# Five reorderings in a hybrid S5 and windowed-attention layer: key products by half tiles, a key power behind a query's, gated columns two units sooner, two scratch buffers swapped, a PSUM ring shifted by one

## The chip, the cores and the metric

The kernel runs on one core of a Trainium2 chip, in one launch. The metric is the device time of that launch in microseconds (us). Three runs gave a median of 1460.14 us (1459.45 to 1464.28). One further execution was profiled; it took 1461.13 us, of which the trace spans 1459.3 us, so that 1.83 us lie around the span.

## The reference, cut to what matters

One encoder layer is computed for two sequences of 512 tokens (width 1024), all in float32. Cut to its data flow:

```python
h = rms_norm(x, ln1)
q, k, v, u, g_att, g_ssm = jnp.split(h @ w_in, IN_SPLITS, axis=-1)
q, k = rms_norm(q per head of 64, q_gain), rms_norm(k per head of 64, k_gain)   # 16 query heads, 4 key heads
y_att = windowed_attention(q, k, v, sink, bias, mask)      # blocks of 128, a block sees its two neighbours
y = gelu(s5(u))                                            # bidirectional state space, 64 groups of 16
y_ssm = y * sigmoid(y @ w_glu + b_glu)
x = x + (sigmoid(g_att) * y_att + sigmoid(g_ssm) * y_ssm) @ w_out
out = x + square(relu(rms_norm(x, ln2) @ w_up)) @ w_down   # inner width 4096
```

## The kernel before, in words

Every float32 product is made of three passes on TensorE (PE): each operand is split into a rounded high part (a CAST on ScalarE, ACT) and the remainder (a subtraction on VectorE, DVE), and high x high, high x low and low x high are added up in one bank of PSUM (`mm3`, L119 to L123). A weight that comes in by DMA can therefore be multiplied only after its CAST and its subtraction. Splits have names in pairs: `c_hi`/`c_lo`, `gc_hi`/`gc_lo`, `w_hi`/`w_lo`, `act0`/`act1`.

The program is one long order written out by hand. Inside a `manual_schedule` the named engines take their instructions exactly in the order of the code; engines that are not named are ordered by a scheduler. All engines take their queues in order, so that an instruction that waits holds back all that stands behind it. Where a DMA is issued from SyncE's queue (SP), the same holds: an issue that waits for a free buffer holds back the issues behind it.

**PSUM before the up phase.** Eight banks: three in the ring `acc()` (L84), two each for `tps` and `sps`, one for `po`. A fourth `acc()` waits until the first one's readers are done. In the up phase (from L1530) the eight banks are handed out again as one ring, `bank()` (L1532).

**The stages the change touches**, in order of time:

1. *Front.* A small product `line` (L509 to L510) takes the bank of `po`, at about 51 us.
2. *Keys of the second half of the tokens* (`key_products`, L219 to L252; 400 to 411.6 us). Four tiles t = 4 to 7 of 128 tokens; each has 24 matmuls of 256 columns into one bank. The key weights come in two halves of 512 columns each, `loaded[len(columns)]` and the next; the second half is split while the first tile runs (`split` at n = 2 and 6). After a tile, ACT squares it (L239), DVE sums (L241), GpSimd (POOL) takes the power -1/2 (L243, L244), and DVE multiplies the keys in the following tile (`later`, L247).
3. *First queries* (L1108 to L1133; 413 to 438 us). For four tiles t = 0 to 3 (T0 to T3 below): the query projection of 24 matmuls (L914), ACT's square (L920), DVE's sum (L924), POOL's add and power (L926, L927), DVE's scaling of the bank to `qn` (L931), four transposes (L936), and the values' product of the same rows (L121 to L123 through `rows_block`). Each tile takes three banks of `acc()` in turn, so a tile's projection goes into the bank of the tile before, and must wait for that tile's `qn`. Between the tiles lies the norm of the first keys, which come back from DRAM: ACT's square `k_sq` (L1120), DVE's sum `k_ms` (L1121), POOL's add and power to `k_rs` (L1122, L1123; 16 numbers a row where a query tile has four), DVE's product with the keys (L1125), POOL's copy `kd` (L883), and four transposes at t = 2 (L896). POOL is not in the manual order here.
4. *Attention* in 8 steps (to about 684 us).
5. *Gated units* (L1305 to L1344; 684 to 754 us). 16 units u; unit u is sequence s = u % 2 of column block m = u // 2. A unit has 24 matmuls (`glu_step`, L128) with the columns of block m, and a string of DVE and ACT work (L804 to L831). The columns of a block come in two pieces (`column_half`, L794), DMA into `c_raw`, CAST to `gc_hi` (L780), subtraction to `gc_lo` (L781). The table `columns` (L1311) says in which unit a piece is loaded and split: blocks 4 to 7 in units 3, 4, 7, 8, 9, 10, 11, 12. The pairs `gc_hi`/`gc_lo` have two buffers, so that block 6's pair takes the place of block 4's. From unit 7 on, the rows of `w_out` are loaded and split as well (`w_raw`, L1297; L1302, L1303).
6. *Out phase* (754 to 856 us). Products with `w_out` (`out_half`), DVE adds `x` (L1376), then the norm: ACT's square (L1393), POOL's power (L1396), DVE's scaling `rn_xn` (L1402), transposes (L1418) for the up phase. Its last products are two pairs of `first_products` for the up phase, read out to `f_sum` (L1449, L1451).
7. *Up phase*, from 856 us: a fast matrix product of seven half-size products a round (L1575 on).

## Time and profile before

| what | value |
|---|---|
| median of three runs | 1460.14 us (1459.45 to 1464.28) |
| profiled execution, its own time | 1461.13 us |
| span of its trace | 1459.3 us |
| around the span | 1.83 us |
| mean granted TensorE clock | 0.999 of full |
| busy DVE, ACT, POOL | 1098.9, 764.3, 236.2 us |
| HBM traffic | 169.02 MB read, 81.82 MB written, 172 GB/s over the span |

A row of the timeline has the start in us, the duration, the engine, the line in the kernel, the operation, output and inputs, the shape, a count of merged instructions, and in brackets the idle time of that engine just before with what ended it. Matmuls overlap: the distance from one start to the next tells the pace, and the duration is longer. A row of the waits has engine, output and line that waited, the engine, output and line waited for, and then the total in us, how often and the longest. A row of the windows has the stretch, its length, each engine's busy time, the granted clock and the DMA share with its rate.

### The profile page before, as it was taken

How to read it: one execution, taken by the hardware profiler on the slowest of the kernel's cores; microseconds unless marked ns; L12 is line 12 of the kernel's file. 1: busy time of each engine (PE TensorE's matmuls, PEld its weight loads, DVE VectorE, ACT ScalarE, POOL GpSimd, SP SyncE). 2: the span in 40 equal slices, each digit the busy share in tenths (PEclk: the TensorE clock that was granted, in tenths of full speed). 3: DMA queues.
4: the chain of work that ended last, by engine and by line, in shares of the span. 5: the costliest groups of instructions: out<-in, count | busy, mean ns of one | idle time of the engine just before them, and what ended most of it. 6: DMA issues, size and time to landing. Idle time of an engine off the chain costs nothing.

```text
span 1459.3 us, 22019 instructions
## 1 busy us (share of the span) xinstructions
PE 1439.5 (99%) x7981; PEld 1226.0 (84%) x7981; DVE 1098.9 (75%) x1985; ACT 764.3 (52%) x1361; POOL 236.2 (16%) x386
## 2 busy tenths in 40 slices
PE   8999999999999999999999999999999999999998
PEld 6788888889999999987788878888888888888887
DVE  6999949995457999988975588777776598475654
ACT  7688861234338887884443355545445444333332
POOL 3144452004244432251100000000000000000000
PEclk9999999999999999999999999999999999999999
DMA  7356549428741533345553245444442993554441
GB/s 277 112 166 182 186 132 340 171 108 291 259 165 47 171 102 102 125 139 173 179 184 114 95 144 183 157 151 144 152 143 103 342 325 111 159 187 147 128 130 58
DMA packets 102204, 240.23 MB, mean 165 GB/s; under 512 B 12330, under 2 KB 25130, under 8 KB 102096
## 3 DMA queue, kind: packets, MB, share of 16 engines
q1 hardware_dynamic: 62160, 139.68, 29.4%
q0 software_dynamic: 16320, 48.28, 10.2%
q10 hardware_dynamic: 23616, 50.87, 9.3%
q8 instruction: 63, 1.03, 0.3%
q14 instruction: 45, 0.37, 0.1%
HBM read 169.02 MB, written 81.82 MB: 172 GB/s over the span
## 4 chain that ended last, share of the span: by engine, by line
PE 87%; DVE 6%; ACT 3%; DMA 1%; issue 1%; POOL 1%; DVEq 0%; ACTq 0%; SPq 0%; POOLq 0%
PE acc L190 16%; PE bank L122 14%; PE bank L121 14%; PE bank L123 14%; PE acc L914 5%; PE acc L123 2%; PE acc L121 2%; PE acc L122 2%; PE acc L128 2%; PE sps L748 2%; PE po L997 2%; PE sps L636 2%; PE sps L965 2%; PE tps L981 2%; PE acc L343 1%
## 5 line engine op out<-in xcount | busy, mean ns | idle before, releaser
L190 PE MATMUL acc<-act,c_hi 128*128 128x512 f32 x768 | 244.1, 395 | 0.0
L122 PE MATMUL bank<-b_lo,a_hi 128*128 128x512 f32 (+1 forms) x449 | 174.7, 389 | 0.0
L123 PE MATMUL bank<-b_hi,a_lo 128*128 128x512 f32 (+1 forms) x449 | 174.5, 389 | 0.0
L121 PE MATMUL bank<-b_hi,a_hi 128*128 128x512 f32 (+1 forms) x449 | 174.5, 389 | 0.0
L190 PEld LDWEIGHTS acc<-act,c_hi 128*128 128x128 f32 x768 | 142.4, 188 | 28.1 <-ACT act L316 0.9
L1649 ACT CAST a_hi<-d_a 128x1024 fp32r<-128x1024 f32 x56 | 59.1, 1055 | 177.9 <-PE bank L122 176.2
L190 PE MATMUL acc<-act,c_lo 128*128 128x512 f32 x384 | 151.2, 394 | 0.0
L121 PE MATMUL bank<-act,act 128*128 128x512 f32 x368 | 143.2, 389 | 2.1 <-ACT act L1410 2.1
L122 PE MATMUL bank<-act,act 128*128 128x512 f32 x368 | 143.2, 389 | 0.0
L123 PE MATMUL bank<-act,act 128*128 128x512 f32 x368 | 143.2, 389 | 0.0
L1650 DVE TENSOR_TENSOR a_lo<-d_a,a_hi 128x1024 fp32r<-128x1024 f32 x56 | 68.5, 1223 | 95.7 <-ACT a_hi L1649 95.7
L914 PE MATMUL acc<-w_hi,act 128*128 128x256 f32 x512 | 115.6, 294 | 1.7 <-DVE qn L931 1.7
L122 PEld LDWEIGHTS bank<-b_lo,a_hi 128*128 128x128 f32 x449 | 84.3, 188 | 18.3 <-DVE b_lo L1650 0.6
L121 PEld LDWEIGHTS bank<-b_hi,a_hi 128*128 128x128 f32 x449 | 84.3, 188 | 17.5
L123 PEld LDWEIGHTS bank<-b_hi,a_lo 128*128 128x128 f32 x449 | 84.3, 188 | 17.1
L914 PEld LDWEIGHTS acc<-w_hi,act 128*128 128x128 f32 x512 | 88.2, 192 | 5.7 <-DVE qn L931 1.9
L190 PEld LDWEIGHTS acc<-act,c_lo 128*128 128x128 f32 x384 | 72.2, 188 | 14.0 <-DVE c_lo L181 0.2
L121 PEld LDWEIGHTS bank<-act,act 128*128 128x128 f32 x368 | 69.1, 188 | 16.8 <-ACT act L1410 2.5
L975 ACT ACTIVATE p<-p,nmx 128x257 f32<-128x257 f32 (+1 forms) x128 | 72.1, 564 | 19.8 <-DVE nmx L969 17.6
L128 PE MATMUL acc<-act,gc_hi 128*128 128x512 f32 x256 | 81.2, 395 | 1.0 <-ACT gc_hi L780 1.0
L123 PEld LDWEIGHTS bank<-act,act 128*128 128x128 f32 x368 | 69.1, 188 | 14.5
L122 PEld LDWEIGHTS bank<-act,act 128*128 128x128 f32 x368 | 69.1, 188 | 14.2
(356 smaller groups left out, 3422.7 us busy)
## 6 DMA issues: line engine op xcount, KB each, us to landing
d_a<-a_scr SPq DMA_DIRECT2D x56, 512.0 KB, 3.6
raws<-in_w_up_dram SPq DMA_DIRECT2D x32, 512.0 KB, 4.1
a_scr<-t ACTq DMA_DIRECT2D x64, 256.0 KB, 3.0
k<-in_w_down_dram SPq DMA_DIRECT2D x32, 512.0 KB, 6.0
c_raw<-in_w_ug_dram SPq DMA_DIRECT2D x48, 256.0 KB, 3.6
ct_scr<-ctab POOLq DMA_DIRECT2D x16, 512.0 KB, 4.6
ctab_in<-ct_scr POOLq DMA_DIRECT2D x16, 512.0 KB, 6.3
a_scr<-a ACTq DMA_DIRECT2D x32, 256.0 KB, 2.0
```

Of the source, the lines that this page charges most:

```text
L121: PE.matmul(ps, a[0], b[0], start=first, stop=False)
L122: PE.matmul(ps, a[0], b[1], start=False, stop=False)
L123: PE.matmul(ps, a[1], b[0], start=False, stop=last)
L128: PE.matmul(ps, w[wi][:, k, :], rows[yi], start=k + p == 0, stop=k == KT - 1 and p == 2)
L190: PE.matmul(ps, w[wi][:, k, :], hT[s][hi][:, k, :], start=n == 0, stop=n == 3 * KT - 1)
L636: PE.matmul(ps[:, i * P:(i + 1) * P], bm[:, ri, g, :], u_sb[:, gp * SH + g, :], start=True, stop=True)
L748: PE.matmul(o, ctab[:, g0 % SI + g, ri, 0:T * CH], st[:, ri, g].rearrange("p s k -> p (s k)"), start=False, stop=ri == 1)
L914: PE.matmul(self.ps, hT[sq][act][:, k, col:col + P], w[:, k % 4, :], start=i == 0, stop=i == 3 * KT - 1)
L965: PE.matmul(ps[:, 0:self.nk], qs, kk[:, self.k0 * P:self.k1 * P], start=i == 0, stop=i == 1)
L975: S.activation(p, p, AF.Exp, bias=self.nmx[:, h:h + 1], scale=-1.0, accum_out=self.sums[:, h, self.qb:self.qb + 1])
L1649: S.copy(hi, src)
L1650: V.tensor_sub(lo, src, hi.bitcast(F32))
```

## The change

What it does, part by part:

- **Keys by half tiles.** Tile 4's first twelve matmuls, then tile 5's first twelve, then the second twelve of each; tiles 6 and 7 as before. Two banks are open at once. `later` comes at n = 17 instead of 12.
- **First keys' power behind a query's.** POOL joins the manual order of the query block, and the add and power of `k_ms`/`k_rs` are written at t = 1 instead of t = 0. With it `k_sq` takes a buffer of the tag `p` instead of `ya`.
- **Gated columns sooner.** Blocks 4 to 7 are loaded and split in units 3 to 10.
- **PSUM ring.** The product `line` takes a bank from `acc()`; the loops that called `acc()` and `bank()` without use, to bring the rings to a fixed place, go.

```diff
     def key_products():
-        later = None
-        for t in range(NB, NT):
-            if t == NB:
+        later, banks = None, {}
+        for t, half in ((4, 0), (5, 0), (4, 1), (5, 1), (6, 0), (6, 1), (7, 0), (7, 1)):
+            if not key_tiles:
                 key_tiles.append(evp.tile([P, 4, N_KV, HD], F32, tag="ev", name="keys"))
-            kt = key_tiles[-1][:, t % 4]
-            ps = acc()[:, 0:CB]
-            for n in range(3 * KT):
+            if not half:
+                banks[t] = acc()[:, 0:CB]
+            ps, kt = banks[t], key_tiles[-1][:, t % 4]
+            for n in range(half * 12, half * 12 + 12):
                 k, p = divmod(n, 3)
-                hi, lo = loaded[len(columns) + k // 4]
+                hi, lo = loaded[len(columns) + half]
...
-                if n == 12 and later:
+                if n == 17 and later:
                     later()
...
+            if not half:
+                continue
...
-        ps = ps_o.tile([P, 512], F32, tag="po", name="line")
+        ps = acc()
         PE.matmul(ps[0:N_HEADS, :], rel_sb, oh_sb, start=True, stop=True)
...
-        with tc.manual_schedule(engines={ET.PE, ET.DVE, ET.Activation}):
+        with tc.manual_schedule(engines={ET.PE, ET.DVE, ET.Activation, ET.Pool}):
...
-                    k_sq = ap.tile([P, NB, N_KV, HD], F32, tag="ya", name="k_sq")
+                    k_sq = ap.tile([P, NB, N_KV, HD], F32, tag="p", name="k_sq", bufs=3)
                     S.activation(k_sq, kn[:, 0:4], AF.Square, scale=HD ** -0.5)
                     V.reduce_sum(ms, k_sq.rearrange("p t h d -> p (t h) d"), axis=AX.X)
+                if t == 1:
                     GP.tensor_scalar_add(ms, ms, EPS)
                     GP.tensor_tensor(rk, ms, neg_half, op=ALU.pow)
-                if t == 1:
                     V.tensor_mul(kn[:, 0:4], kn[:, 0:4],
...
-        columns = {u: (4 + i // 2, i % 2) for i, u in enumerate((3, 4, 7, 8, 9, 10, 11, 12))}
+        columns = {u: (4 + i // 2, i % 2) for i, u in enumerate(range(3, 11))}
...
-        while banks_used[0] % 3 != 1:
-            acc()
...
-    for _ in range(6):
-        bank()
```

What the code's move makes of the engines' queues, at three places. First TensorE in the key products; `acc_4365` is the bank of tile 4, `c_hi_4179`/`c_lo_4180` the first half of the weights and `c_hi_4369`/`c_lo_4370` the second. Before, from tile 4's last matmul with the first half on:

```order
L230 MATMUL acc_4365<-c_hi_4179,act1_107 128x256
L230 MATMUL acc_4365<-c_hi_4369,act0_106 128x256
L230 MATMUL acc_4365<-c_lo_4370,act0_106 128x256
L230 MATMUL acc_4365<-c_hi_4369,act1_107 128x256
L230 MATMUL acc_4365<-c_hi_4369,act0_106 128x256
```

And in the change, where `acc_4384` is the bank of tile 5:

```order
L227 MATMUL acc_4365<-c_hi_4179,act1_107 128x256
L227 MATMUL acc_4384<-c_hi_4179,act0_106 128x256
L227 MATMUL acc_4384<-c_lo_4180,act0_106 128x256
L227 MATMUL acc_4384<-c_hi_4179,act1_107 128x256
...
L227 MATMUL acc_4365<-c_hi_4369,act0_106 128x256
L227 MATMUL acc_4365<-c_lo_4370,act0_106 128x256
```

Tile 5's twelve matmuls with the first half now stand between the two halves of tile 4.

Second GpSimd in the first queries, where a pair of `ms` and `rq` belongs to one query tile, from T0's power on. Before:

```order
L927 TENSOR_TENSOR rq<-ms,neg_half 128x4
L1122 TENSOR_SCALAR k_ms<-k_ms 128x16
L1123 TENSOR_TENSOR k_rs<-k_ms,neg_half 128x16
L926 TENSOR_SCALAR ms<-ms 128x4
L927 TENSOR_TENSOR rq<-ms,neg_half 128x4
L883 COPY kd<-kn 128x512
L926 TENSOR_SCALAR ms<-ms 128x4
```

And in the change:

```order
L926 TENSOR_TENSOR rq<-ms,neg_half 128x4
L956 COPY p<-vec 128x4
L925 TENSOR_SCALAR ms<-ms 128x4
L926 TENSOR_TENSOR rq<-ms,neg_half 128x4
L1122 TENSOR_SCALAR k_ms<-k_ms 128x16
L1123 TENSOR_TENSOR k_rs<-k_ms,neg_half 128x16
L882 COPY kd<-kn 128x512
L925 TENSOR_SCALAR ms<-ms 128x4
```

The keys' two instructions have changed places with T1's two; the copy `kd` still follows, ahead of T2's pair. The small copy `p` (a first attention unit's) comes between T0 and T1.

Third VectorE in units 4 to 7 of the gated stage, where a unit ends with its L831 and its pieces of weights follow. Before, from unit 4's end on:

```order
L831 TENSOR_TENSOR act_8302<-ga,act_8301 128x512
L781 TENSOR_TENSOR gc_lo<-c_raw,gc_hi 128x512
...
L831 TENSOR_TENSOR act_8304<-ga,act_8303 128x512
L825 TENSOR_TENSOR ga<-ga,gs 128x512
...
L831 TENSOR_TENSOR act_8302<-ga,act_8301 128x512
L825 TENSOR_TENSOR ga<-ga,gs 128x512
...
L831 TENSOR_TENSOR act_8304<-ga,act_8303 128x512
L781 TENSOR_TENSOR gc_lo<-c_raw,gc_hi 128x512
L1303 TENSOR_TENSOR act_8300<-w_raw,act_8299 128x512
```

And in the change:

```order
L830 TENSOR_TENSOR act_8302<-ga,act_8301 128x512
L780 TENSOR_TENSOR gc_lo<-c_raw,gc_hi 128x512
...
L830 TENSOR_TENSOR act_8304<-ga,act_8303 128x512
L780 TENSOR_TENSOR gc_lo<-c_raw,gc_hi 128x512
...
L830 TENSOR_TENSOR act_8302<-ga,act_8301 128x512
L780 TENSOR_TENSOR gc_lo<-c_raw,gc_hi 128x512
...
L830 TENSOR_TENSOR act_8304<-ga,act_8303 128x512
L780 TENSOR_TENSOR gc_lo<-c_raw,gc_hi 128x512
L1302 TENSOR_TENSOR act_8300<-w_raw,act_8299 128x512
```

Units 5 and 6 get a split each, block 5's; the split in unit 7 is now block 6's. ACT's casts and SP's loads of `c_raw` move along; units 11 and 12 lose theirs.

More of the change, by code (lines that the diff above doesn't have):

```diff
@@ L78, in hybrid_layer @@
     opers = ExitStack()
-    given = itertools.count()
-    banks_used = [0]
     def acc():
-        banks_used[0] = next(given) + 1
         return ps_acc.tile([P, 512], F32, tag="acc", name="acc")
```

## The prediction

> **What bounds the kernel now.** The page first: TensorE is busy almost throughout, so only time in which it stands still, or steps slowly, can be won.
>
> ```profile
> PE 1439.5 (99%) x7981; PEld 1226.0 (84%) x7981; DVE 1098.9 (75%) x1985; ACT 764.3 (52%) x1361; POOL 236.2 (16%) x386
> ```
>
> Of the 1459.3 us span that leaves 19.8 us of idle PE. The waits of PE say where, and the rows that bear on the change are these:
>
> ```profile
> PE bank L121 <- ACT act L1410: 2.1, 1, 2.1
> PE acc L914 <- DVE qn L931: 1.7, 1, 1.7
> PE acc L128 <- ACT gc_hi L780: 1.0, 1, 1.0
> PE acc L128 <- DVE gc_lo L781: 0.7, 1, 0.7
> ```
>
> Each happens once; together they make 5.5 us, and the two of the key products below add 0.6. A wait's idle time understates its cost, since the last matmul before it drains and the first ones after it step slowly; so I price by start-to-start distances in the timeline, less the usual step. A reading of this kernel tells about 0.3% (4.4 us) from no change.
>
> **Keys by half tiles.** The timeline of PE, ACT and DVE at the second half of the key weights:
>
> ```profile
> 401.26 0.28 PE L230 MATMUL acc<-c_lo,act 128*128 128x256 f32 x1
> 401.38 0.28 PE L230 MATMUL acc<-c_hi,act 128*128 128x256 f32 x1
> 401.92 0.38 PE L230 MATMUL acc<-c_hi,act 128*128 128x256 f32 x1 [0.26 <-ACT c_hi L180]
> 402.64 0.39 PE L230 MATMUL acc<-c_lo,act 128*128 128x256 f32 x1 [0.34 <-DVE c_lo L181]
> 402.87 0.41 PE L230 MATMUL acc<-c_hi,act 128*128 128x256 f32 x2
> 401.25 1.14 ACT L180 CAST c_hi<-c_raw 128x512 fp32r<-128x512 f32 x2 [0.40 <-ACT sg L205]
> 401.90 1.29 DVE L181 TENSOR_TENSOR c_lo<-c_raw,c_hi 128x512 fp32r<-128x512 f32 x2 [9.16 <-ACT c_hi L180]
> ```
>
> A step is 0.12 us (401.26 to 401.38). From 401.38 to 402.87 three steps take 1.49 us, 1.13 too much. In the change twelve matmuls of tile 5 lie in between, 12 x 0.12 = 1.44 us, so the second halves begin at 401.38 + 0.12 + 1.44 = 402.94. The first `c_lo` comes out half way through the DVE row of two, 401.90 + 0.65 = 402.55; the cover is enough by 0.4. The second is done at 403.19, and wanted six steps after the first. Gain 1.1 (between 0.9 and 1.1). Keys are now scaled five steps (0.6 us) later in a tile; the bank that this frees is wanted thirty matmuls (3.6 us) after it: nothing.
>
> **First keys' power behind a query's.** Timeline around T1 and T2, and the windows' row of the stretch behind:
>
> ```profile
> 421.68 2.92 POOL L1123 TENSOR_TENSOR k_rs<-k_ms,neg_half 128x16 f32<-128x16 f32 x1
> 421.96 0.42 DVE L924 TENSOR_REDUCE ms<-sq 128x4 f32<-128x256 f32 x1 [0.71 <-ACT sq L920]
> 424.54 0.28 PE L123 MATMUL acc<-w_hi,act 128*128 128x256 f32 x1
> 424.69 0.23 POOL L926 TENSOR_SCALAR ms<-ms 128x4 f32<-128x4 f32 x1
> 425.00 1.04 POOL L927 TENSOR_TENSOR rq<-ms,neg_half 128x4 f32<-128x4 f32 x1
> 426.07 0.42 DVE L931 TENSOR_TENSOR qn<-acc,rq 128x256 f32<-128x256 f32 x1 [3.69 <-POOL rq L927]
> 426.55 0.39 PE L914 MATMUL acc<-w_hi,act 128*128 128x256 f32 x1 [1.74 <-DVE qn L931]
> 427.64 1.22 DVE L1125 TENSOR_TENSOR kn<-kn,k_rs 128x1024 f32<-128x1024 f32 x1
> 428.78 1.22 DVE L1129 TENSOR_TENSOR va<-vn,va 128x1024 fp32r<-128x1024 f32 x1
> 429.00 1.47 POOL L883 COPY kd<-kn 128x512 f32<-128x512 f32 x1 [2.96 <-DVE kn L1125]
> 434.69 0.36 PE L914 MATMUL acc<-w_hi,act 128*128 128x256 f32 x1
> 427.60:431.02 3.42, 3.42 (x19) 3.40 (x18) 2.40 (x3) 0.00 (x0) 1.47 (x1) 0.50 0.00 0
> ```
>
> T1's sum is done at 422.38, but its power waits on POOL behind the keys' 2.92 us; so T2's first matmul, which needs T1's bank, starts 2.01 us after the last one, 1.89 too late. Right behind it the granted clock is 0.50 for 3.42 us: some 16 query matmuls at 0.21 instead of 0.12, about 1.5 us more. I put that down to the stop, which is the only one near.
>
> In the change, all 1.1 us earlier: sum done 421.3, add 0.3, power 1.04, `qn` at 422.65, and 0.48 later (as 426.07 to 426.55) T2 may start, 423.1; PE gets there at 424.54 + 0.12 - 1.1 = 423.56. No stop: 1.89 + 1.5 = 3.4 gained.
>
> What becomes late next is T2's own power. POOL now runs the keys' add and power from 422.65 to about 426.0; DVE's key product to 427.1, and behind it in DVE's queue the values' subtraction to 428.3; T2's sum stands behind both and ends at 428.7, though its projection is done by 426.5. POOL copies `kd` from 427.3 to 428.8, then T2's add and power end at 430.2, and T3 may start at 430.7. It is due at 423.56 plus the distance of T2 to T3 before without its slow clock, 434.69 - 426.55 - 1.5 = 6.6, so at 430.2: 0.5 us of new wait (0, if POOL and DVE hand over faster, to 1.0, if sum and copy do not overlap). `kd` itself is done at 428.8, one microsecond before its transposes. Net 2.9 (2.4 to 3.4). `k_sq` in `p` instead of `ya` adds no instruction; the buffer it takes held half of the values' weights, whose splits precede the first value product: nothing.
>
> **Gated columns sooner.** Timeline, and the windows' row of 700 to 740 us:
>
> ```profile
> 712.37 0.61 PE L128 MATMUL acc<-act,gc_hi 128*128 128x512 f32 x2
> ...
> 716.64 0.73 PE L128 MATMUL acc<-act,gc_hi 128*128 128x512 f32 x2 [0.96 <-ACT gc_hi L780]
> 718.10 0.50 PE L128 MATMUL acc<-act,gc_lo 128*128 128x512 f32 x1 [0.73 <-DVE gc_lo L781]
> 718.43 0.62 PE L128 MATMUL acc<-act,gc_hi 128*128 128x512 f32 x2
> 712.35 0.69 DVE L781 TENSOR_TENSOR gc_lo<-c_raw,gc_hi 128x512 fp32r<-128x512 f32 x1
> 715.97 0.62 ACT L780 CAST gc_hi<-c_raw 128x512 fp32r<-128x512 f32 x1 [0.28 <-DMA c_raw<-in_w_glu_dram]
> 700.00:740.00 40.00, 38.21 (x167) 30.65 (x166) 38.56 (x56) 20.31 (x35) 4.24 (x8) 1.00 0.53 180
> 767.74 1.29 DVE L1402 SCALAR_TENSOR_TENSOR rn_xn<-x,rs,ln_bc 128x1024 f32<-128x1024 f32 x1 [2.58 <-POOL rs L1396]
> 769.46 1.03 PE L1418 MATMUL tps<-ident,rn_xn 128*128 128x128 f32 x8
> ```
>
> Block 5's first product starts at 712.37, and its fifteen matmuls up to 718.43 take 6.06 us against 15 x 0.23 = 3.4: 2.6 lost. With the splits in units 5 and 6 the weights lie ready: that goes. (The clock reads 1.00 over these 40 us though PE stops for 0.96 in them, so the 0.5 at T3 should not slow it either.) But DVE is busy 38.56 of these 40 us, and the edit only moves its work: two splits (0.6 us a step) come two units sooner, two leave units 11 and 12. DVE itself can win at most the 1.44 us in which it stands; and it can lose, because block 6's pair takes block 4's place, so that unit 7's cast must wait for PE's last product of block 4, which ends at 712.37, just where DVE's split stands (712.35), and then takes 0.62 itself: up to 0.9 on DVE. So PE leaves the stage 2.6 us earlier on its own account, DVE between 0.9 later and 1.4 earlier. They meet at the first transposes of the out phase: `rn_xn` is done at 767.74 + 1.29 = 769.03, PE wants it at 769.46. PE can run ahead of DVE's chain by 0.43 us more and no further. So the edit yields 0.43 plus what DVE wins, -0.5 to 1.9, and I take 0.4, DVE's own gain as nought, since its queue is full. The rest comes back as a wait of some 2 us before the transposes near 767 us.
>
> **PSUM ring.** Timeline of PE, DVE and ACT where the up phase starts, and the windows' row behind it:
>
> ```profile
> 853.57 0.39 PE L123 MATMUL acc<-act,act 128*128 128x512 f32 x1
> 856.11 0.47 PE L121 MATMUL bank<-act,act 128*128 128x512 f32 x1 [2.15 <-ACT act L1410]
> 855.28 0.68 DVE L1449 TENSOR_TENSOR f_sum<-acc,f_sum 128x512 f32<-128x512 f32 x1
> 858.85 0.68 DVE L1437 TENSOR_TENSOR tx<-tx,tps 128x512 f32<-128x512 f32 x1
> 855.40 0.62 ACT L1410 CAST act<-tx 128x512 fp32r<-128x512 f32 x1 [1.36 <-DVE tx L1432]
> 856.50:860.00 3.50, 3.50 (x17) 2.92 (x16) 2.73 (x5) 2.11 (x4) 0.00 (x0) 1.00 0.41 131
> ```
>
> 2.54 us lie between two starts, 2.3 too much. The row names ACT's cast, which ends at 856.02; but that is the operand of the third product (T2), while the first one's (B22) is long split. The bank ring's first bank is the one that the last `first_products` was summed into, and DVE reads it out at 855.28 to 855.96. With `line` in the ring, every later bank of `acc` is one place on, and the first bank was read out two products earlier. The first product can start at 853.80. Next to bind is the third, at 853.80 + 24 x 0.2275 = 859.26, whose bank is read until 858.85 + 0.68 = 859.53: 0.3. Net 2.0 (1.7 to 2.3). `line` itself now shares a ring of three at 51 us: no row shows its wait; I take 0, and 0.3 at most, as for the key weights.
>
> **Sum.** 1.1 + 2.9 + 0.4 + 2.0 = 6.4: the profiled 1461.13 would be 1454.7, its span 1452.9. The median before is 1.0 below the profiled execution: 1460.14 - 6.4 = 1453.7.
>
> **The rivals.**
>
> *The gated stage's gain stays.* DVE wins its 1.4, or the norm's chain comes earlier with the `x` loads: 2.6 instead of 0.4, 1451.5. For it speaks that DVE stands 1.44 us in the stage; against, the full queue. 0.15.
>
> *The half clock stays or moves.* If the slow 3.42 us do not hang on the 1.74 us stop, or if the new stop near 767 us draws the same, 1.5 come back: 1455.2. For it: that stop would be as long as the one before the slow stretch; against: behind the 2.15 us stop at 856 us the clock reads 1.00 (856.5 to 860). 0.12. [...]
>
> *The keys' power only hands the wait on.* If T3 stops as T2 did (1.9 and the clock's 1.5), the second edit yields nothing: 1456.6. For it: the same 2.92 us lie on POOL, and what hangs on them now holds T2's sum and power on DVE and POOL; against: it starts a tile's power earlier than T3's need, and the working above leaves 0.5, not 1.9. 0.12.
>
> *The ring does not do what it says.* If ACT's cast was the true releaser, the 2.0 stay: 1455.7. For it: the row's own name, and ends 0.06 us apart; against: what the cast writes is used later. 0.06.
>
> *Slower: ACT and DVE stand for PE in the gated stage.* The casts of blocks 6 and 7 wait for PE's last product of blocks 4 and 5, and everything behind them on ACT (the next gates) and DVE with them. If ACT gets there a whole product early, each costs 24 x 0.2275 = 5.5 us of a full DVE, twice: 10.9 - 6.0 from the other edits is 4.9 slower, 1465.0. It decides when ACT reaches unit 7's cast 4 or more us ahead of PE's last matmul of block 4; in the trace unit 7's split on DVE and the end of that product are level (712.35, 712.37). 0.05.
>
> **How the numbers follow.** The forecast has 0.50. The terms' bounds add up to 0.9 + 2.4 - 0.5 + 1.7 = 4.5 at the least and 1.1 + 3.4 + 1.9 + 2.3 = 8.7 at the most: 1451.4 to 1455.6. The rivals but the slower one reach to 1456.6, and a median of a few runs moves by 0.7 (the lowest run before lies 0.7 under its median): 1450.6 to 1457.2. Faster by over 4.4 us means below 1455.8: nearly all of the forecast and the first rival (0.63), two thirds of the clock's case, half of the ring's and little of the third: 0.75. Slower 0.05, the rest 0.20.
>
> **What would show it.** PE without a wait at 400 to 403 and before T2; clock 1.00 through 423 to 431; a wait of about 0.5 at T3, on `qn`; no wait on `gc_hi`/`gc_lo`, an ACT wait on PE in unit 7, and a PE wait on `rn_xn` of about 2 us near 763; the first `bank` matmul 0.23 after the last `acc`. Wrong if T3 waits more than 1 us, the clock still falls, or the stop before the transposes is missing or over 2.5.

## The result, and the profile after

The changed kernel takes 1452.1 us (median of four runs, 1451.57 to 1454.8); the kernel before, in the same job, 1461.25 (1459.45 to 1464.28). The ratio is 0.9939 with an interval of 0.9917 to 0.9961: faster by 0.6%, more than the 0.3% that can be told (the kernel before's four runs lie 0.33% apart). The profiled execution took 1452.05 us with a span of 1450.3, against 1461.13 and 1459.3. Below, two of the twelve runs of e11, 1503.83 and 2414.14 us at granted clocks of 0.911 and 0.557, are left out of its median.

To see where the 9 us come from, take the start of the same TensorE matmul in both traces and subtract. What a stretch gained is the difference between two rows.

| place | before, us | after minus before, us | gained since the row above |
|---|---|---|---|
| ahead of the key products | 389.83 | -0.18 | (start of the program) |
| behind the two halves of tiles 4 and 5 | 404.18 | -1.29 | 1.11 keys |
| T3's first query matmul | 434.69 | -3.98 | 2.69 queries |
| gated stage, block 5 | 711.24 | -3.91 | -0.07 |
| the same block, fifteen matmuls on | 718.43 | -6.57 | 2.66 columns |
| transposes of the out phase | 770.25 | -6.59 | 0.02 |
| end of the out phase | 840 | -6.56 | -0.03 |
| up phase, behind the first products | 862 | -8.57 | 2.01 ring |
| middle of the up/down phase | 1205 | -9.02 | 0.45 |
| near the end | 1440 | -9.05 | 0.03 |

Against the forecast's 1.1, 2.9, 0.4 and 2.0, only the columns stand out: their whole 2.66 us was kept, where 0.4 was expected to be left behind the transposes.

The waits of PE after:

```profile
PE acc L913 <- DVE qn L930: 0.5, 1, 0.5
...
PE bank L117 <- DVE tx L1436: 0.3, 1, 0.3
```

All four waits shown before are gone: 2.1 at the up phase, 1.0 and 0.7 in the gated stage, 1.7 on `qn` at T2. The 0.5 on `qn` is a new one, at T3, and so is the 0.3 on a bank of the up phase. No wait on `rn_xn` has come.

Keys, on PE and DVE:

```profile
402.65 0.40 PE L227 MATMUL acc<-c_hi,act 128*128 128x256 f32 x2
402.89 0.28 PE L227 MATMUL acc<-c_lo,act 128*128 128x256 f32 x1
401.74 1.29 DVE L177 TENSOR_TENSOR c_lo<-c_raw,c_hi 128x512 fp32r<-128x512 f32 x2 [9.11 <-ACT c_hi L176]
```

The row of 402.65 holds tile 5's last matmul with the first half of the weights and tile 4's first with the second, without a bracket. DVE's two subtractions, 401.74 to 403.03, now run while PE works on tile 5's first half: the first is done near 402.39 (half of the row), and its `c_lo` is wanted at 402.89.

The queries, where the tiles' powers and the keys' stand on POOL, and T2 and T3 begin:

```profile
421.49 1.04 POOL L926 TENSOR_TENSOR rq<-ms,neg_half 128x4 f32<-128x4 f32 x1
422.96 2.93 POOL L1123 TENSOR_TENSOR k_rs<-k_ms,neg_half 128x16 f32<-128x16 f32 x1
427.29 1.47 POOL L882 COPY kd<-kn 128x512 f32<-128x512 f32 x1 [1.39 <-DVE kn L1124]
429.16 1.04 POOL L926 TENSOR_TENSOR rq<-ms,neg_half 128x4 f32<-128x4 f32 x1
428.21 0.41 DVE L923 TENSOR_REDUCE ms<-sq 128x4 f32<-128x256 f32 x1
423.25 0.28 PE L119 MATMUL acc<-w_hi,act 128*128 128x256 f32 x1
423.37 0.28 PE L913 MATMUL acc<-w_hi,act 128*128 128x256 f32 x1
430.71 0.39 PE L913 MATMUL acc<-w_hi,act 128*128 128x256 f32 x1 [0.55 <-DVE qn L930]
424.00:432.00 8.00, 7.45 (x64) 7.22 (x62) 4.79 (x8) 3.01 (x5) 4.64 (x4) 1.00 0.00 0
```

T2 starts 0.12 behind the last matmul (forecast 423.56, read 423.37). T3 is held for 0.55 by `qn`, through the chain sum 428.21, copy to 428.76, power 429.16 to 430.20; it starts at 430.71 (forecast 430.7). The last row is the windows' row: clock 1.00 where before 3.42 us ran at half.

The gated stage and the out phase. First the rows of before that answer to it and were not needed earlier: DVE's `yy` at the stage's start, DVE's splits of two rows of `w_out`, and the loads that follow them up to ACT's first cast of the up weights:

```profile
690.03 1.14 DVE L807 TENSOR_TENSOR yy<-act,act 128x512 f32<-128x512 f32 x1 [1.35 <-DMA mix_scr<-ya]
...
753.73 1.28 DVE L1303 TENSOR_TENSOR act<-w_raw,act 128x512 fp32r<-128x512 f32 x2
754.44 1.64 SPq L1297 DMA_DIRECT2D w_raw<-in_w_out_dram  x2
756.66 0.84 SPq L1385 DMA_DIRECT2D f_raw<-in_w_up_dram  x2
762.61 1.19 ACT L1386 CAST f_hi<-f_raw 128x512 fp32r<-128x512 f32 x2 [2.39 <-DMA f_raw<-in_w_up_dram]
```

And after:

```profile
684.69 1.15 DVE L806 TENSOR_TENSOR yy<-act,act 128x512 f32<-128x512 f32 x1
708.43 0.62 ACT L779 CAST gc_hi<-c_raw 128x512 fp32r<-128x512 f32 x1 [1.89 <-PE acc L124]
709.09 0.69 DVE L780 TENSOR_TENSOR gc_lo<-c_raw,gc_hi 128x512 fp32r<-128x512 f32 x1 [0.80 <-ACT gc_hi L779]
700.00:740.00 40.00, 40.00 (x179) 33.10 (x178) 37.40 (x54) 20.73 (x36) 3.18 (x6) 1.00 0.56 193
748.93 1.29 DVE L1302 TENSOR_TENSOR act<-w_raw,act 128x512 fp32r<-128x512 f32 x2
749.64 0.93 SPq L1296 DMA_DIRECT2D w_raw<-in_w_out_dram  x2
751.15 0.85 SPq L1384 DMA_DIRECT2D f_raw<-in_w_up_dram  x2
756.29 1.21 ACT L1385 CAST f_hi<-f_raw 128x512 fp32r<-128x512 f32 x2 [1.38 <-DMA f_raw<-in_w_up_dram]
761.42 1.28 DVE L1401 SCALAR_TENSOR_TENSOR rn_xn<-x,rs,ln_bc 128x1024 f32<-128x1024 f32 x1 [2.58 <-POOL rs L1395]
762.87 1.04 PE L1417 MATMUL tps<-ident,rn_xn 128*128 128x128 f32 x8
```

PE is busy in all 40 us (38.21 before). Unit 7's cast does wait for PE's last product of block 4 (1.89), which costs DVE 0.80, as foreseen. But `rn_xn` begins at 761.42, 6.32 earlier than before, and is done at 762.70; PE's transposes start at 762.87 without a wait. The two still meet, with 0.17 to spare. `yy` no longer waits for a DMA, and `f_raw` is issued 5.51 earlier. That issue stands in SP's queue behind two loads `w_raw`, each of which waits for one of DVE's two splits to free its buffer: the first is issued 0.71 behind the start of DVE's row, before and after.

The ring:

```profile
846.86 0.39 PE L119 MATMUL acc<-act,act 128*128 128x512 f32 x1
847.09 0.39 PE L117 MATMUL bank<-act,act 128*128 128x512 f32 x1
852.97 0.47 PE L117 MATMUL bank<-act,act 128*128 128x512 f32 x1 [0.28 <-DVE tx L1436]
```

0.23 between the two starts instead of 2.54; the third product waits 0.28 for its bank (0.3 was worked out).

### The profile page after: what moved, and what is told of

Same layout as the page of the kernel before. It is cut to its first block, busy times and chain, and to the rows that moved or that the text cites. A ratio compares the mean times of both kernels' runs of the same rounds, so it can differ in the third digit from the quotient of the medians.

```text
span 1450.3 us, 22020 instructions
## 1 busy us (share of the span) xinstructions
PE 1436.3 (99%) x7981; PEld 1224.7 (84%) x7981; DVE 1098.3 (76%) x1985; ACT 763.9 (53%) x1361; POOL 234.7 (16%) x386
## 3 DMA queue, kind: packets, MB, share of 16 engines
q8 instruction: 63, 1.03, 0.3%
## 4 chain that ended last, share of the span: by engine, by line
PE 86%; DVE 4%; ACT 3%; issue 2%; POOL 2%; DMA 1%; SPq 0%; DVEq 0%; POOLq 0%; ACTq 0%
PE acc L186 15%; PE bank L117 14%; PE bank L118 14%; PE bank L119 14%; PE acc L124 5%; PE acc L913 5%; PE acc L119 2%; PE acc L118 2%; PE acc L117 2%; PE po L996 2%; PE sps L635 2%; PE sps L964 2%; PE tps L980 2%; PE acc L342 1%; PE tps L604 1%
```

## The experiments

Twelve kernels were run. "After plus" stands for the changed kernel with one edit, "before plus" for the kernel before with one edit. The table gives each one's time with its ratio to the kernel before on the same chip, and, from the profiled executions, the lead over the profile of before at nine places (negative is earlier). The profiles stand up to 2.3 us apart before these stages begin (the first column; PE's first wait alone, for operands of the first loads, takes 5.5 to 6.6 us by run); so a gain is read as the difference of two columns.

| run | median us | ratio [interval] | 390 | 404 | 435 | 711 | 718 | 770 | 862 | 1205 | 1440 |
|---|---|---|---|---|---|---|---|---|---|---|---|
| changed kernel | 1452.1 | 0.9939 [0.9917, 0.9961] | -0.18 | -1.29 | -3.98 | -3.91 | -6.57 | -6.59 | -8.57 | -9.02 | -9.05 |
| e1_after_rows_back | 1452.05 | 0.9934 [0.9919, 0.9949] | -1.66 | -2.84 | -5.55 | -5.51 | -8.17 | -6.23 | -8.47 | -8.83 | -8.86 |
| e2_columns_alone | 1459.06 | 0.9992 [0.9980, 1.0003] | -0.60 | -0.54 | -0.53 | -0.53 | -3.19 | -1.68 | -2.05 | -0.58 | -0.59 |
| e3_columns_and_rows | 1459.15 | 0.9986 [0.9976, 0.9996] | -0.25 | -0.23 | -0.23 | -0.23 | -2.90 | -1.48 | -1.83 | -0.42 | -0.45 |
| e4_query_order_alone | 1460.36 | 0.9986 [0.9972, 1.0000] | -1.81 | -1.79 | -4.50 | -4.46 | -4.36 | -4.36 | -2.87 | -0.38 | -0.39 |
| e5_ring_alone | 1458.69 | 0.9981 [0.9972, 0.9991] | -1.77 | -1.82 | -1.84 | -1.84 | -1.93 | -1.89 | -4.09 | -4.36 | -4.40 |
| e6_keys_alone | 1459.34 | 0.9991 [0.9982, 1.0000] | -1.66 | -2.77 | -2.74 | -2.72 | -2.66 | -2.65 | -3.00 | -1.92 | -1.95 |
| e7_after_norm_later | 1454.66 | 0.9959 [0.9944, 0.9974] | 0.00 | -1.18 | -3.88 | -3.87 | -6.54 | -2.82 | -3.49 | -3.90 | -3.93 |
| e8_after_t3 | 1452.03 | 0.9933 [0.9919, 0.9946] | -1.23 | -2.33 | -5.82 | -5.80 | -8.46 | -6.82 | -9.03 | -8.11 | -8.12 |
| e9_after_first_weights_later | 1454.05 | 0.9950 [0.9938, 0.9963] | -2.27 | -3.37 | -6.07 | -5.97 | -8.64 | -8.65 | -9.97 | -7.34 | -7.36 |
| e10_after_t3_and_weights_later | 1451.69 | 0.9934 [0.9922, 0.9946] | -1.51 | -2.68 | -6.17 | -6.11 | -8.78 | -8.80 | -10.16 | -9.56 | -9.57 |
| e11_columns_and_weights_later | 1459.10 | 0.9983 [0.9974, 0.9992] | -1.02 | -0.92 | -0.91 | -0.81 | -3.47 | -3.50 | -1.31 | -1.53 | -1.52 |
| e12_after_t3_and_gain_later | 1450.49 | 0.9930 [0.9917, 0.9944] | -1.64 | -2.69 | -6.18 | -6.11 | -8.77 | -8.79 | -10.64 | -10.59 | -10.61 |

**Why did the columns' gain stay?** Two theories stood against each other. The first: `k_sq` in `p` turns the rotation of the `ya` buffers by one, so that `yy`, a tile over their old memory, waits for an earlier DMA than the last; that sets DVE's chain ahead and with it `rn_xn`. The second: the swap has no part in it. The first three runs put the swap back, and try the columns with and without it.

### e1_after_rows_back

```diff
-                    k_sq = ap.tile([P, NB, N_KV, HD], F32, tag="p", name="k_sq", bufs=3)
+                    k_sq = ap.tile([P, NB, N_KV, HD], F32, tag="ya", name="k_sq")
```

> The changed kernel with k_sq back in the tag ya, all else kept. Theory A (the swap of the rows' buffers turns the memory of yy over to the attention's last but one ya, so that VectorE no longer waits for the DMA of the last one): the 1.35 us wait of yy for that DMA is back near 686, VectorE's chain comes 1.3 us later to the scaling before the first transposes of the out phase, and TensorE waits there 1.0 to 1.4 us; span about 1.2 above the changed kernel's 1450.3. Rival B (the wait was gone by the DMA's own luck): no wait at yy or the same as in the changed kernel, TensorE's lead at 770 unchanged, span within 0.4 of it.

```profile
684.53 1.14 DVE L806 TENSOR_TENSOR yy<-act,act 128x512 f32<-128x512 f32 x1 [1.35 <-DMA mix_scr<-ya]
...
756.71 1.22 ACT L1385 CAST f_hi<-f_raw 128x512 fp32r<-128x512 f32 x2 [3.01 <-DMA f_raw<-in_w_up_dram]
761.83 1.28 DVE L1401 SCALAR_TENSOR_TENSOR rn_xn<-x,rs,ln_bc 128x1024 f32<-128x1024 f32 x1 [2.58 <-POOL rs L1395]
763.17 1.09 PE L1417 MATMUL tps<-ident,rn_xn 128*128 128x128 f32 x8 [1.75 <-DVE rn_xn L1401]
```

The wait of `yy` is back, 1.35 us to the hundredth, so the swap removes that wait: shown. PE also stops before the transposes, and 1.94 of the 2.66 go. Yet the time is the same, because the profiled run stood 1.5 us earlier all the way to there; at the transposes it and the changed kernel are level (-6.23 and -6.59). That looks less like a wait handed down than like a date at which `rn_xn` is ready, whenever PE comes.

### e2_columns_alone

```diff
-        columns = {u: (4 + i // 2, i % 2) for i, u in enumerate((3, 4, 7, 8, 9, 10, 11, 12))}
+        columns = {u: (4 + i // 2, i % 2) for i, u in enumerate(range(3, 11))}
```

> The kernel before with only the gated columns two units sooner. Forecast's step (VectorE's full queue gives the gain back): TensorE is 2.6 us ahead at 720 and waits about 2 us before the first transposes near 767, so that 0.4 to 1.2 is left at 850. Rival (the gain stays by itself): 2.5 us ahead at 850, no wait before the transposes.

```profile
761.25 1.23 ACT L1386 CAST f_hi<-f_raw 128x512 fp32r<-128x512 f32 x2 [3.11 <-DMA f_raw<-in_w_up_dram]
766.38 1.28 DVE L1402 SCALAR_TENSOR_TENSOR rn_xn<-x,rs,ln_bc 128x1024 f32<-128x1024 f32 x1 [2.58 <-POOL rs L1396]
767.72 1.09 PE L1418 MATMUL tps<-ident,rn_xn 128*128 128x128 f32 x8 [1.32 <-DVE rn_xn L1402]
```

Alone, the columns win 2.66 and keep 1.15 behind the transposes, inside the 0.4 to 1.2 expected. The stop that the forecast put there is there, 1.32 us long where about 2 was expected. By 1205 us the rest is lost too, in the down phase (last section). The time is not told apart from before.

### e3_columns_and_rows

The edit of e2, and `k_sq` in `p`.

> The kernel before with the gated columns two units sooner and k_sq in the tag p. Theory A: yy no longer waits 1.35 us near 690, and TensorE keeps 1.3 us more of its lead at 850 than with the columns alone. Rival B: the same lead as with the columns alone, within 0.3.

`yy` does not wait in this run and starts 1.67 us earlier than before, but the columns keep 1.25 (-0.23 to -1.48), against 1.15 in e2: the swap is worth 0.1. What it sets DVE ahead is taken back once ACT and DVE have waited for PE's products in units 7 and 9: at the twelfth `yy` (724.9 in before) DVE stands 1.31 later than in before, in e2 1.02. So the first theory is half right, and fails as an explanation: the wait goes, but the gain at the transposes doesn't come from it.

**A third theory: the load of `f_raw`.** In all of before, after, e1, e2 and e3, `rn_xn` begins 5.12 or 5.13 us after ACT's first cast of `f_raw` (before 762.61 and 767.74, after 756.29 and 761.42, e2 761.25 and 766.38), and sooner in no run that loads `f_raw` ahead of the norm. This cast and its subtraction stand in ACT's and DVE's queues ahead of the first norm, and wait for a DMA that the norm doesn't need. From its issue to the cast it is 5.95 us before, 5.14 after, 6.00 in e1, 6.43 in e2, 6.61 in e3. By this theory the earliest date of the transposes is that cast plus 5.13, plus 1.34 for PE.

### e7_after_norm_later

A test of what a late norm costs: the first `f_lo` subtraction is done three times over, the same numbers each time.

```diff
-            V.tensor_sub(lo, raw, hi.bitcast(F32))
+            for _ in range(3):
+                V.tensor_sub(lo, raw, hi.bitcast(F32))
```

> The changed kernel with each f_lo subtraction of the first up-phase weights done three times, which puts 4 x 0.6 = 2.4 us more on VectorE ahead of the norm before the first transposes of the out phase. If that chain just meets TensorE there (the forecast's bound: TensorE cannot run ahead of it), TensorE waits 2.0 to 2.4 us for the scaling rn_xn and the span grows by as much. Rival (the chain has slack, so the gated stage's gain was never in danger): a wait under 1.0.

```profile
766.33 1.45 PE L1418 MATMUL tps<-ident,rn_xn 128*128 128x128 f32 x8 [3.27 <-DVE rn_xn L1402]
...
766.92:770.34 3.42, 3.42 (x12) 2.85 (x11) 1.38 (x2) 2.22 (x4) 0.72 (x2) 0.50 0.84 298
```

PE stops for 3.27 where 2.0 to 2.4 was expected, the transposes come 3.46 later than in the changed kernel (766.33 and 762.87), and the granted clock falls to 0.50 for 3.42 us behind the stop. Of the 3.46, 1.92 are the repeated subtractions (7.05 from the cast to `rn_xn` instead of 5.13) and 1.65 a later cast (757.94 against 756.29), which the edit does not explain: the load took 6.57 here. Some 2.4 us of added work thus delayed the norm by 1.92, so there is little room behind `f_lo`. At the end the profile has lost 4.9 us against the changed kernel, counted from 390; in the median it is 2.6 (1454.66 against 1452.1).

### e11_columns_and_weights_later

The decisive run: e2, with the load of `f_raw` and its splits moved out of the first norm's way. A copy of one column of the second norm's output into the buffer keeps the load from being issued before that norm is done.

```diff
             raw = rn2.tile([P, 4, P], F32, tag="w_raw", name="f_raw", bufs=3)
+            GP.tensor_copy(raw[:, 0, 0:1], owed[2][:, 0:1])
             SP.dma_start(raw, w_up[r, :, i])
...
-        ws = [up_parts(0, i, ...) for i in range(2)]
         for t in range(NT // 2):
...
+            if t == 1:
+                ws = [up_parts(0, i, ...) for i in range(2)]
```

> The kernel before with the gated columns two units sooner (as e2) and the first up-phase weights later (as e9). Theory F: the 1.3 us wait of e2 before the transposes goes, and of the 2.5 us won at 712 to 718 all is left at 850. Rival (a full VectorE queue gives it back, as the forecast had it): a wait of 1 us or more stays there.

```profile
763.99 1.28 DVE L1403 SCALAR_TENSOR_TENSOR rn_xn<-x,rs,ln_bc 128x1024 f32<-128x1024 f32 x1 [2.58 <-POOL rs L1397]
765.97 1.04 PE L1419 MATMUL tps<-ident,rn_xn 128*128 128x128 f32 x8
```

`rn_xn` begins 2.39 earlier than in e2, PE doesn't wait, and the lead goes through unchanged (-3.47, -3.50): all 2.66 are kept, against 1.15 in e2. What gave the columns' gain back was the load ahead of the norm: shown. The total does not gain, and the expectation that all is left at 850 fails: the splits now stand ahead of a later norm, whose transposes near 785 us wait 0.9, and 1.25 go behind the up phase's 2.1 us stop (the lead between 840 and 862 falling from -2.56 to -1.31), close to the 1.49 that go there in e4 at a clock of 0.50.

### e9_after_first_weights_later

The same edit on the changed kernel.

> The changed kernel with the first two weights of the up phase (f_raw) loaded and split after the first norm's scaling: their load is issued behind the second rn_xn, by a one-column copy on GpSimd that it must wait for. Theory F (what decides whether the gated stage's 2.5 us stay is the landing of f_raw, 5.1 to 6.6 us after its issue, ahead of the norm on ACT and VectorE): the scaling rn_xn comes 2 to 3 us earlier than without, TensorE has no wait before the transposes whatever the start of the run, its lead over the kernel before at 770 is the whole of that at 720, and the median is 0.5 to 1.5 under the changed kernel's 1452.1. Rival (the chain is held by the loads of w_out or x in any case): rn_xn comes less than 0.7 earlier, and a wait of TensorE stays in a run that starts early.

```profile
760.81 1.04 PE L1418 MATMUL tps<-ident,rn_xn 128*128 128x128 f32 x8
```

A wait of PE in the same run:

```profile
PE tps L1418 <- DVE rn_xn L1402: 0.9, 1, 0.9
```

The lead passes whole (-8.64, -8.65), here from a start 2.1 us earlier than the changed kernel's, where e1 lost 1.94. The expected time, 0.5 to 1.5 under the changed kernel's 1452.1, was missed at 1454.05: the splits of `f_raw` now hold that later norm (0.9), and the down phase gives back 2.6.

**Each remaining edit by itself.** Three runs check the other terms of the sum.

### e4_query_order_alone

POOL in the manual order, and `GP.tensor_scalar_add`/`GP.tensor_tensor(rk, ...)` from t == 0 to t == 1; `k_sq` stays in `ya`.

> The kernel before with only the keys' power behind T1's on GpSimd (k_sq stays in ya). Forecast's step: no wait of T2, clock 1.00 from 423 to 432, a wait of about 0.5 at T3, TensorE 2.9 us ahead from 435 on (2.4 to 3.4), and still that at 850. Rival (the half clock does not hang on the stop): the slow stretch of 3.4 us is still there near 427 and the lead is 1.4.

```profile
423.00:432.00 9.00, 8.47 (x72) 8.23 (x71) 5.59 (x9) 3.45 (x6) 5.12 (x4) 1.00 0.00 0
...
851.80:855.22 3.42, 3.42 (x9) 2.65 (x9) 2.92 (x5) 2.03 (x5) 0.00 (x0) 0.50 0.37 103
```

Its waits of PE:

```profile
PE bank L121 <- ACT act L1410: 2.1, 1, 2.1
PE bank L122 <- DVE b_lo L1650: 1.8, 3, 0.7
...
PE acc L914 <- DVE qn L931: 0.5, 1, 0.5
```

The query block wins 2.71 with the clock at 1.00, and T3 waits 0.5: the forecast's working, to 0.2. But the up phase's stop of 2.1 us, harmless in before, is now followed by a half clock (1.49 lost), and 2.5 go in the down phase, where PE waits 1.8 for `b_lo`. At the end the profile stands 0.39 ahead, though it was 1.81 ahead before the query block.

### e5_ring_alone

`line` from `acc()`, the two loops gone.

> The kernel before with only the PSUM ring shifted. Forecast's step: the first product of the up phase starts 0.23 us after the last acc matmul, the third waits 0.3, TensorE 2.0 ahead at 862 (1.7 to 2.3). Rival (the cast was the true releaser): the 2.15 us wait stays, no lead. On the down phase, where e2 to e4 lost 1.4 to 2.7 us of lead between 1170 and 1200 to weights by DMA: theory C (they lose it because the ring is not shifted there) keeps the 2.0 at 1200; theory D (the loads have no slack there, whatever the ring) leaves less than 1.0.

```profile
851.35 0.39 PE L123 MATMUL acc<-act,act 128*128 128x512 f32 x1
851.58 0.39 PE L121 MATMUL bank<-act,act 128*128 128x512 f32 x1
```

0.23 between the starts: the bank was what was waited for, not ACT's cast that the row of before names, which in this run begins at 853.18, 1.60 behind the product. 2.20 us (-1.89 to -4.09), kept to the end.

### e6_keys_alone

The new `key_products`.

> The kernel before with only the keys by half tiles. Forecast's step: no wait of TensorE between 400 and 404, 1.1 us ahead at 410 (0.9 to 1.1), still so at 850. Rival: the second half's splits are later than 402.94 and a wait of 0.3 or more stays, 0.7 ahead or less. In the down phase: theory C or D as for the ring alone, 1.1 at 1200 for neither under C, since the ring is not shifted, and under D less than 0.5.

1.11 us at the keys (-1.66 to -2.77), to the hundredth as in the whole change; 1.1 lost again in the down phase.

**Can the rest be had?** The three last runs build on the changed kernel.

### e8_after_t3

The 0.5 us at T3 hangs on POOL's copy `kd` and on the values' subtraction ahead of T2's sum. Here DVE makes `kd`, and the values' split comes a tile later.

```diff
-                    kd = key_copies(0, 0)
-                    S.copy(va[:, 0:4, :, 0:HD], vn)
-                    V.tensor_sub(va[:, 0:4, :, HD:P], vn, va[:, 0:4, :, 0:HD].bitcast(F32))
+                    kd = ap.tile([P, 4, 2, HD], F32, tag="qn", name="kd")
+                    V.tensor_copy(kd, kn[:, 0:4, 0, None, :].to_broadcast([P, 4, 2, HD]))
                 if t == 2:
                     key_turn(0, 0, kd)
+                    S.copy(va[:, 0:4, :, 0:HD], vn)
+                    V.tensor_sub(va[:, 0:4, :, HD:P], vn, va[:, 0:4, :, 0:HD].bitcast(F32))
```

> The changed kernel with the copy kd on VectorE instead of GpSimd and the split of the first values moved from t = 1 to t = 2. By the working for T3 (GpSimd's copy and VectorE's subtraction hold T2's power): T2's sum ends near 428, its power near 429.5, and T3's 0.5 us wait goes, span 0.4 to 0.6 under the changed kernel's. Rival (T3 waits for the keys' power alone): the wait stays.

```profile
756.12 1.22 ACT L1386 CAST f_hi<-f_raw 128x512 fp32r<-128x512 f32 x2 [3.47 <-DMA f_raw<-in_w_up_dram]
...
762.59 1.09 PE L1418 MATMUL tps<-ident,rn_xn 128*128 128x128 f32 x8 [1.46 <-DVE rn_xn L1402]
```

The queries win 3.49 instead of 2.69 (T3 is not held), and 1.64 are given back at the transposes: again `f_raw` plus 5.13. Time unchanged. The edit moves both at once, so it does not tell the copy's part from the subtraction's.

### e10_after_t3_and_weights_later

e8 and e9 together.

> Both edits to the changed kernel: T3's power freed (e8) and the first up-phase weights later (e9). Theory F: e8's 0.7 at T3 is no longer given back before the transposes, so the median is 1.0 to 2.2 under the changed kernel's 1452.1, without a wait of TensorE at T3 or before the transposes. Rival: e8's gain goes back there or in the down phase, median within 0.7 of 1452.1.

Both gains pass the transposes (-8.78, -8.80), 0.9 goes at the later norm. 1451.69 us (1451.43 to 1452.3), by the ratio level with the changed kernel: the 1.0 to 2.2 that were expected did not come.

### e12_after_t3_and_gain_later

If the load must stay ahead of the norm, let it be issued sooner: the 512 KB broadcast of the norm's gain stood ahead of it in SP's queue.

```diff
         x1s = [load_rows_of(sq, 0) for sq in range(NSEQ)]
-        SP.dma_start(ln2_bc, ln2.to_broadcast([P, D]))
...
         ws = [up_parts(0, i, ...) for i in range(2)]
+        SP.dma_start(ln2_bc, ln2.to_broadcast([P, D]))
```

on top of e8.

> e8's kernel with the load of the norm's gain ln_bc (512 KB, broadcast over the partitions) issued behind the two loads f_raw instead of ahead of them. Theory F (f_raw's landing decides): ACT's cast of f_raw starts 4.0 to 5.0 us after f_raw's issue instead of 5.1 to 6.6, TensorE's wait before the transposes is under 0.5 even in a run that starts early, e8's 0.7 at T3 is kept to 840, median 0.5 to 1.5 under the changed kernel's 1452.1. Rival (the landing hangs on the loads of w_out and x before it, or ln_bc now comes too late for the scaling): cast 5 us or more after the issue, or a wait of 1 us or more, median within 0.5 of 1452.1. In the down phase each profile may lose 0 to 2.9 us to loads of w_down, for either.

```profile
748.47 0.85 SPq L1385 DMA_DIRECT2D f_raw<-in_w_up_dram  x2
753.89 1.35 ACT L1386 CAST f_hi<-f_raw 128x512 fp32r<-128x512 f32 x2 [2.17 <-DMA f_raw<-in_w_up_dram]
759.14 1.28 DVE L1402 SCALAR_TENSOR_TENSOR rn_xn<-x,rs,ln_bc 128x1024 f32<-128x1024 f32 x1 [2.58 <-POOL rs L1396]
760.67 1.04 PE L1418 MATMUL tps<-ident,rn_xn 128*128 128x128 f32 x8
```

The load is issued 1.27 sooner than in e8, but 0.81 of that is DVE's splits of `w_out`, which came sooner in this run (their loads are issued at 747.43 against 748.24); the edit's own part is 0.46, the place of the broadcast in the queue. The load still takes 5.42 to the cast, where 4.0 to 5.0 was expected. The cast comes 2.23 earlier, PE doesn't wait, the lead passes (-8.77, -8.79) and stays to the end (-10.61). The time is 1450.49 us, 1450.01 to 1450.73 over five runs, the lowest of all here; the changed kernel's four runs lie at 1451.57 or above. But the kernel before was 1.45 lower in that job too (1459.8), and the ratios' intervals overlap. Nor do the traces show a gain in all: this profile was 1.46 further ahead at 390 already, and from there to 1440 it wins 8.97 against the changed kernel's 8.87. T3's 0.7 passes the transposes, and most of it goes again in the down phase, where the changed kernel won 0.45 and this one lost 0.05.

## Why the prediction was right, point by point

- **Keys: 1.1, measured 1.11**, in the whole change and alone. The cover of twelve matmuls was enough.
- **Queries: 2.9, measured 2.69** (2.71 alone). T2 without a wait; T3 held 0.55, at 430.71 as worked out; e8, where it goes, shows that the hold was the copy, the subtraction or both. From start to start the hold costs 0.8 (3.49 less 2.69), which is the 0.2 missing. The clock's 1.5 us went with the stop, in this run and in e4.
- **Columns: 0.4, measured 2.66.** The gain in the gated stage was right (2.6); the step that failed is "DVE's own gain as nought, since its queue is full". PE and DVE's chain do meet at the transposes, as it was put, and PE could not have run ahead of it; but the chain came 6.32 us earlier, not the 4.0 of keys and queries, and PE did not have to wait. The prediction had named a missing stop before the transposes as a sign that it is wrong; the stop is missing, so by its own sign this part is wrong.
- **Columns, why the chain came sooner.** What dates its end is the load of `f_raw` ahead of the norm (e2 against e11), a transfer that the forecast's working does not have, and that load's issue waits in turn for DVE's splits of `w_out`. So the 6.32 are three parts: the splits came 4.80 earlier (753.73 to 748.93), SP's queue was 0.71 shorter (in before the second `w_raw` took 1.04 us to issue, in after 0.33), and the load landed 0.81 faster. Of the 4.80, 3.91 were there when the stage began; DVE's own gain was 0.89, inside the forecast's -0.9 to 1.4. By the forecast's rule, 0.43 plus that gain, 1.3 would have been kept; the other half of the 2.66 came by the queue and the landing. The other runs with the same splits bear this out: DVE's own gain, the queue's 0.7, the landing against before's and the 0.38 by which PE could still run ahead (in before the transposes start 1.72 behind `rn_xn`, where PE waits 1.34) add up to 0.77 in e1, 1.21 in e2, 1.31 in e3 and 1.07 in e8, and kept were 0.72, 1.15, 1.25 and 1.02. The landing is no property of the change: with before's 5.95 us from issue to cast, `rn_xn` would have been 0.81 later, past the 0.17 that were spare, and about 0.6 us would have come back. Over the runs that load `f_raw` ahead of the norm it took 5.05 to 6.61 us; how much of that is chance and how much the traffic around it, one profile of each kernel doesn't settle. The stop that was put at some 2 us came in e1 (1.75), e2 (1.32) and e8 (1.46), and the changed kernel just missed it, in part by luck.
- **`k_sq` in `p`, priced at nothing:** it removed a wait of 1.35 us on DVE that the forecast had not looked for (e1 and e3). On PE it is worth about 0.1 by e2 and e3, one profile of each.
- **Ring: 2.0, measured 2.01** (2.20 alone), the third product's 0.28 included. The forecast's step of 0.2275 was an estimate; the bank's products step by 0.227 (847.09 to 852.30 in 23 steps). The rival that ACT's cast releases it is refuted by e5.
- **The rivals.** That the gated gain stays (0.15) is what happened, and partly for each of its reasons: DVE won 0.89 of its 1.4, and the chain came earlier with a load, though with `f_raw` and not with `x`. That ACT and DVE stand for PE: the waits came (1.89 on ACT, 0.80 on DVE), but on a part of a product, not on a whole one. The half clock did not stay, T3 did not take over the wait, and the ring did what it says.
- **The clock.** T2's stop of 1.9 us and the half clock behind it went together. Over 420 to 435 us the granted clock reads 0.89 in before, e2 and e3, which have the stop (a wait of 1.7 each), and 1.00 in the change, e1 and e4, which don't. In e5, e6 and e11, which have it too, the lead stays within 0.03 from 404 to 435, so that this stretch took as long as in before, the slow steps included.
- **Sum:** 6.4 forecast, 9.05 in the traces: 2.3 from the columns, 0.45 from the down phase and 0.18 from the start. That is more than the 8.7 that the terms' bounds add up to; from the 1460.14 that the forecast started from it would be 1451.1. The median of 1452.1 stands above the 1451.4 of those bounds only because the kernel before took 1461.25 in this job. The edits run alone win 2.71, 2.66, 2.20 and 1.11, or 8.7, at their places, and end their profiles between 1.4 later (e4) and 2.6 earlier (e5) than they began; by time they make 0.14, 0.08, 0.19 and 0.09%, together 0.5 of the 0.6%. Of the four intervals, e2's reaches past 1 and those of e4 and e6 reach up to it, so only e5 is clearly told apart from before.

## What to carry to other kernels

Where a small edit's gain has to pass a later meeting of two engines, follow the other engine's chain back to the transfer that dates it, and see what that transfer's issue waits for and whether it moves with the edit: that a queue is busy throughout does not yet say when the chain behind it ends (here DVE worked 38.56 of 40 us, and its chain came 6.32 earlier). A load that stood ahead of the norm, which doesn't need it, dated the norm: `rn_xn` began 5.12 or 5.13 us behind that load's cast in before, after, e1, e2 and e3. Moving it freed the work here (e9 to e11; in e11 `rn_xn` began 2.39 earlier than in e2), but in none of these runs did that show in the time. And a tile's memory brought its former users' waits with it, so that a buffer swap that adds no instruction took a wait away and brought it back (1.35 us on `yy`, gone in the change, back in e1).

## What the runs showed of the hardware

**When the clock halves.** The half clocks that have a row of their own lasted 3.42 us each: from 427.60 in before, 851.80 in e4 and 766.92 in e7. A step of the query matmuls took 0.21 there in before instead of 0.12, one of the up phase 0.43 in e4 instead of 0.23. What brings it, the stops of PE tell only in part; here they are counted from start to start, less the usual step. T2's stop, 1.89 us in before and a wait of 1.7 in all six profiles that have it, was followed by a half clock in before, e2 and e3 (0.89 over 420 to 435 us), and e5, e6 and e11 take as long there. The stop at the up phase, 2.31 us in before and in e4, and a wait of 2.1 in both as in e2, e3, e6 and e11, was followed by one in e4 (0.86 over 850 to 862 us) and by none in before, e2 and e3 (1.00); in e11 1.25 us went at this place, and in e6 none (-2.65 at 770, -3.00 at 862). e7's stop of 3.43 was followed by one. Stops of 1.48 (e2), 1.62 (e8) and 1.90 (e1) before the transposes were not: the matmuls behind them step by 0.23. So a stop's length does not decide alone, since 2.31 in before brought nothing and 1.89 at T2 did; what else counts stays open. The same wait at the up phase thus cost 1.2 to 1.5 us more (1.25 in e11, 1.49 in e4) or nothing.

**The down phase.** Seven of thirteen profiles lost 0.6 to 2.6 us of lead between 1150 and 1205 us, six lost none. There DVE waits for the `w_down` loads, in e2:

```profile
1186.71 3.50 DVE L1644 TENSOR_TENSOR k<-k,k 128x1024 f32<-128x1024 f32 x3 [2.52 <-DMA k<-in_w_down_dram]
```

and in before:

```profile
1187.26 3.50 DVE L1644 TENSOR_TENSOR k<-k,k 128x1024 f32<-128x1024 f32 x3 [1.03 <-DMA k<-in_w_down_dram]
```

2.52 us of waiting against 1.03 on the same load. It hits kernels with and without each of the edits (e2, e3, e4, e6, e8, e9, e10); what tips it stays open.
